# A depthwise convolution in 40 overlapping chunks, and half-sums made in another order

## The chip, the cores and the metric

The kernel runs on one core of one Trainium2 chip. TensorE (PE in the rows) multiplies matrices, VectorE (DVE) and ScalarE (ACT) read its results and do the elementwise work, GpSimd (POOL) helps and starts some of the transfers, SyncE (SP) starts the others. The metric is the device time of one execution in microseconds. Before the change it was 1102.43 us, the median of 3 runs (1102.43 to 1102.51).

## The reference

It is one layer of a streaming encoder over 640 tokens of width 1024: one prompt of 512 and 8 samples of 16, each sample with a state of its own.

```
z = x @ w_in                                    # 6656 columns: xa, ya, glu, q, three gates
out_a = (rg_lru(conv4(xa)) * gelu(ya)) @ proj_a
u = glu[..., :512] * sigmoid(glu[..., 512:])
v = causal_depthwise_conv(concat(conv_b_prev, u), conv_b_w, conv_b_b)     # 31 taps, 512 channels
out_b = silu(layer_norm(v, ln_b_g, ln_b_b)) @ proj_b
out_c = mem_cross_attention(q, k, v) @ proj_c
merged = g[0] * out_a + g[1] * out_b + g[2] * out_c
x = layer_norm(alpha * x + merged @ w_out)
x = layer_norm(alpha * x + (silu(x @ w_ffn_gate) * (x @ w_ffn_up)) @ w_ffn_down)
```

Layer norms before the layer, the memory's projections and the new states of both convolutions are computed too. The prompt's convolution starts from zeros, that of a sample from its 30 earlier rows.

## The kernel before

Activations lie with channels on the 128 partitions and the 640 tokens along the row, in the tiles `xh` and `xl`. Every product is made in three passes, since a number is kept as a high and a low part of a short format: high x high, high x low, low x high. A weight block of 128 output channels is loaded by SP's queue (`wr`), its high part is copied by ScalarE (`wh`), its low part is subtracted by VectorE (`wl`, some by POOL), and TensorE makes two 320-column accumulations of it (`pu`), which ScalarE and VectorE read.

The program is a list of such steps in a fixed order: memory projections, the GLU blocks, the queries, the gates, `proj_c`, `proj_b`, the first gate's pairs, `proj_a`, the output projection, the FFN pairs, the down projection. All compute instructions go through one helper, so their line is L64. Background streams (the convolution, attention, the LayerNorm of the second branch, the scan, the half-sums) are generators. While a step's instructions are written out, a planner sums prices for VectorE, ScalarE and TensorE (`price_vector`, L75, and its neighbours) and lets streams go on as long as VectorE and ScalarE are priced ahead of TensorE; `finish` and `flush` run a stream to its end where its result is needed. So each engine's order follows from the prices, and a cheaper price moves work of several streams.

The second branch's convolution is `conv_b_stream` (L810). For each of four blocks of 128 channels, `conv_b_taps` (L796) starts an accumulator `v` on ScalarE and then adds 30 taps on VectorE with two instructions each: one over the prompt's columns, shifted, of 511 down to 482 columns, and one of 8 x 16 columns over the samples, which lie in a history tile of 8 x 46 columns. `ln_b_stream` (L850) sums the four blocks on POOL (L853, L855), and TensorE sums over channels with a matrix of ones (`pv<-s,ones`).

The gate pairs and the FFN's gate and up projections take two 128-column blocks at once, with seven products in place of eight (`seven`, L1464; the list `PRODUCTS`, L1459). The products need four sums of quarters of x, s1 to s4, made by `sums_stream` (L1386) on VectorE, and sums of weight quarters, t1 to t4 (`Pair`, L1429). Each product is 12 matmuls of 320 columns; its `put` reads the accumulators, and `through` (L1525) applies the gate's function on ScalarE. All of s1 to s4 are finished in the hook before the second product of the first pair. Before the down projection, `before_down` (L1709) splits the first two blocks of the FFN's hidden layer into high and low parts (`split_h`, L1701), one copy on ScalarE and one subtraction on VectorE each. Tiles of 128 x 640 come from 52 slots (`Slots`, L110).

## Time and profile before

| | |
|---|---|
| median of 3 runs | 1102.43 us |
| the profiled execution | 1102.82 us |
| its span | 1101.1 us |
| TensorE busy | 1064.1 us, 97% |
| VectorE busy | 799.0 us, 73% |
| ScalarE busy | 486.9 us, 44% |
| GpSimd busy | 165.0 us, 15% |
| granted TensorE clock, mean | 0.989 |

A row of a timeline is a run of like instructions: start, duration in us, engine and line, operation, what is written from what, shape, count, and in brackets the idle time of the engine before it with the instruction that ended it. In a run the duration reaches from the first start to the last end. Names: `s` a slot's tile, `pu` and `pv` accumulators, `pb` and `pa` per-channel parameters, `wr`, `wh`, `wl` a weight block as loaded, its high and its low part. "Granted clock" is the share of TensorE's full speed that the throttle allowed in a window.

### The profile page before, as it was taken

Reading aid. Unit: us, or ns where it says so; the run is one execution under the profiler, and the core shown is the slowest. Engines: PE = TensorE matmul, PEld = TensorE weight load, DVE = VectorE, ACT = ScalarE, POOL = GpSimd, SP = SyncE. Lnnn points to the kernel's source line nnn. Section 1 sums busy time; section 2 is a strip of 40 time slices with the busy share of each in tenths; the row PEclk is TensorE's granted clock in tenths of the full one; section 3 lists DMA queues with packets and bytes.
Section 4 is the critical chain, followed back from the end, with each engine's and each line's share of the span. In section 5 each row is a group of like instructions: output and inputs, shape, how many; then the busy total and the mean of one; then the engine's idle time right before and its main releaser. Section 6 shows DMA issues by size and latency. Waiting matters only on the chain.

```text
span 1101.1 us, 16991 instructions
## 1 busy us (share of the span) xinstructions
PE 1064.1 (97%) x6827; PEld 1007.0 (91%) x6827; DVE 799.0 (73%) x1333; ACT 486.9 (44%) x861; POOL 165.0 (15%) x185
## 2 busy tenths in 40 slices
PE   8799898998999999999999999999999999999997
PEld 6699898997999999999999889899999999788886
DVE  6929898994465865699655579888887887544775
ACT  4532545445648346646423023444444443344341
POOL 3623323556200000010001120000000000100111
PEclk9999999998999999999999999999999999999999
DMA  9732123353313113212325431222233222734481
GB/s 339 252 95 78 39 67 96 118 154 94 118 39 96 59 58 115 78 44 77 115 78 172 148 120 59 71 82 78 77 95 97 77 77 86 278 115 132 165 294 39
DMA packets 80334, 123.11 MB, mean 112 GB/s; under 512 B 4075, under 2 KB 59371, under 8 KB 80256
## 3 DMA queue, kind: packets, MB, share of 16 engines
q1 hardware_dynamic: 73168, 100.36, 27.6%
q0 software_dynamic: 7088, 21.68, 6.3%
q8 instruction: 53, 0.87, 0.3%
q14 instruction: 25, 0.20, 0.1%
HBM read 112.41 MB, written 9.61 MB: 111 GB/s over the span
## 4 chain that ended last, share of the span: by engine, by line
PE 76%; DVE 14%; ACT 3%; issue 2%; POOL 2%; DMA 1%; SPq 0%; DVEq 0%; ACTq 0%; POOLq 0%
PE pu L64 67%; DVE s L64 12%; PE pv L64 9%; ACT s L64 2%; DVE wl L64 1%; ACT L64 1%; POOL s L540 1%; POOL s L541 1%; DMA s<-in_w_mem_k 0%; ACT wh L64 0%; DMA wr<-in_w_ffn_down 0%; DMA s<-in_x_prompt 0%; DVE xres L64 0%; DVE xl L64 0%; DVE mx L64 0%
## 5 line engine op out<-in xcount | busy, mean ns | idle before, releaser
L64 PE MATMUL pu<-xh,wh 128*128 128x320 f32 x1040 | 251.7, 314 | 4.6 <-ACT s L64 3.0
L64 PE MATMUL pu<-xh,wl 128*128 128x320 f32 x1040 | 246.9, 310 | 0.0
L64 ACT ACTIVATE wh<-wr 128x1024 fp32r<-128x1024 f32 (+1 forms) x149 | 135.1, 908 | 236.8 <-PE pu L64 139.0
L64 PE MATMUL pu<-xl,wh 128*128 128x320 f32 x888 | 219.4, 310 | 0.0
L64 PE MATMUL pu<-s,wh 128*128 128x320 f32 x1064 | 185.7, 310 | 1.6 <-ACT s L64 1.1
L64 PEld LDWEIGHTS pu<-xh,wh 128*128 128x128 f32 x1040 | 177.6, 189 | 9.4 <-ACT s L64 3.8
L64 PEld LDWEIGHTS pu<-xh,wl 128*128 128x128 f32 x1040 | 177.5, 189 | 0.0
L64 DVE TENSOR_TENSOR s<-s,s 128x640 fp32r<-128x640 f32 (+4 forms) x176 | 124.1, 723 | 62.4 <-ACT s L64 57.2
L64 PEld LDWEIGHTS pu<-s,wh 128*128 128x128 f32 x1064 | 163.4, 188 | 3.0 <-ACT s L64 1.7
L64 DVE TENSOR_TENSOR wl<-wr,wh 128x1024 fp32r<-128x1024 f32 (+1 forms) x100 | 114.1, 1142 | 67.6 <-ACT wh L64 67.6
L64 PEld LDWEIGHTS pu<-xl,wh 128*128 128x128 f32 x888 | 154.0, 189 | 0.6 <-DVE xl L64 0.6
L64 PE MATMUL pu<-s,wl 128*128 128x320 f32 x808 | 148.6, 311 | 2.8 <-ACT s L64 1.6
L64 DVE TENSOR_TENSOR s<-s,pu 128x320 f32<-128x320 f32 x186 | 87.8, 484 | 79.9 <-PE pu L64 77.1
L64 DVE SCALAR_TENSOR_TENSOR s<-s,pb,s 128x511 f32<-128x511 f32 (+14 forms) x240 | 130.1, 614 | 7.8 <-ACT s L64 7.8
L64 PEld LDWEIGHTS pu<-s,wl 128*128 128x128 f32 x808 | 126.6, 189 | 3.8 <-DVE s L64 1.9
L64 ACT ACTIVATE s<-s 128x640 fp32r<-128x640 f32 (+4 forms) x144 | 86.9, 628 | 97.2 <-DVE s L64 94.7
L64 PE MATMUL pu<-wh,s 128*128 128x512 f32 (+1 forms) x396 | 117.6, 390 | 3.0 <-ACT s L64 2.6
L64 PEld LDWEIGHTS pu<-wh,s 128*128 128x128 f32 x396 | 73.8, 191 | 18.2 <-ACT s L64 2.9
L64 ACT ACTIVATE s<-pu 128x320 f32<-128x320 f32 (+2 forms) x90 | 36.7, 442 | 75.5 <-PE pu L64 75.5
L64 PE MATMUL pu<-wl,s 128*128 128x512 f32 (+1 forms) x198 | 63.3, 391 | 1.5 <-POOL wl L305 0.8
L305 POOL TENSOR_TENSOR wl<-wr,wh 128x1024 fp32r<-128x1024 f32 x13 | 44.4, 3414 | 83.1 <-ACT wh L64 70.3
L64 PE MATMUL pv<-wh,s 128*128 128x512 f32 (+1 forms) x152 | 48.7, 368 | 0.4 <-DVE xres L64 0.4
(139 smaller groups left out, 1241.6 us busy)
## 6 DMA issues: line engine op xcount, KB each, us to landing
wr<-in_w_in SPq DMA_DIRECT2D x26, 1024.0 KB, 5.2
wr<-in_w_ffn_down SPq DMA_DIRECT2D x19, 1024.0 KB, 5.0
wr<-in_w_ffn_gate SPq DMA_DIRECT2D x11, 1024.0 KB, 5.4
wr<-in_w_ffn_up SPq DMA_DIRECT2D x11, 1024.0 KB, 5.4
s<-in_cache_mem_k POOLq DMA_DIRECT2D x16, 256.0 KB, 7.4
s<-in_cache_mem_v POOLq DMA_DIRECT2D x16, 256.0 KB, 6.9
wr<-in_proj_a SPq DMA_DIRECT2D x4, 1024.0 KB
wr<-in_w_out SPq DMA_DIRECT2D x4, 1024.0 KB, 5.9
```

The lines of the kernel that those rows point to most:

```text
L64: return f(*a, **k)
L305: self.eng.tensor_tensor(l, x, f32(h), op=OP.subtract)
L540: G.tensor_tensor(y[1], y[1], g[1], op=OP.mult)
L541: G.tensor_tensor(y[1], y[1], b[1], op=OP.add)
```

## The change

The history tiles become one tile per block of channels, `u0` to `u3`, of 40 chunks with 46 columns each: 32 chunks of the prompt and 8 of the samples, each with its 30 earlier columns and 16 of its own. Two memsets on POOL clear the history of the prompt's first two chunks. VectorE writes the GLU's product straight into the chunks' last 16 columns in two instructions of 20 x 16, and ScalarE copies the earlier columns: 31 x 16, 30 x 14 and, for the new states, 128 and 30 columns. A tap is then one instruction of 40 x 16 = 640 columns, so 120 instead of 240.

When a block's convolution is done, its tile is used again as three parts (`m0` to `m3` in the rows), which `get` gives out first for high and low parts; the slots go from 52 to 40.

The sums stream makes the wholes and mixtures of 22, 21 and 11 for both halves first, then the parts of s2 and s3, s1 where it does not overwrite a quarter of x, then 12 and s4. The first pair of each group takes its products in the order m1, m4, m2, m6, m7, m5, m3, with m4's `put` delayed until m7's; a product that needs a sum first calls `sum_there`, which runs the stream to that sum. The first two calls of `split_h` move from `before_down` into hooks before the fifth and fourth step from the end of the FFN pairs.

```diff
-NSLOT = 52
+NSLOT = 40
...
             def evac_a(p, k=k):
-                u = sg.pop(k)
-                each(V.tensor_mul, u, two(u), p)
-                copy(us[k][:, :, 30:46], u[:, TP:].rearrange("p (b t) -> p b t", t=TS))
-                up[k] = u
+                u = us[k]
+                for c in range(2):
+                    V.tensor_mul(u[:, 20 * c:20 * c + 20, 30:46],
+                                 *(y.rearrange("p (c n) -> p c n", n=TS) for y in (c2(sg[k])[:, c], p[c])))
+                free(sg.pop(k))
+                copy(u[:, 1:32, 14:30], u[:, 0:31, 30:46])
+                copy(u[:, 2:32, 0:14], u[:, 0:30, 32:46])
+                if k == 0:
+                    up[0] = get([128, KC, 160])
+                copy(up[0][:, k, :128].rearrange("p (b t) -> p b t", t=TS), u[:, 32:, 30:46])
+                copy(up[0][:, k, 128:158], u[:, 31, 16:46])
                 uready.append(k)
...
         for j in range(29, -1, -1):
-            s = 30 - j
-            V.scalar_tensor_tensor(v[:, s:TP], u[:, :TP - s], w(j), v[:, s:TP], op0=OP.mult, op1=OP.add)
-            V.scalar_tensor_tensor(vs, h[:, :, j:j + 16], w(j), vs, op0=OP.mult, op1=OP.add)
+            V.scalar_tensor_tensor(v3, h[:, :, j:j + 16], w(j), v3, op0=OP.mult, op1=OP.add)
             yield "v" if j else 1
...
+        yield from part("s2", "11", True)
+        yield from part("s3", "21")
+        if in_place is None:
+            yield from part("s1", "22")
+        for i in blocks:
+            whole("12", i)
+            yield "v"
+            mix("12", "12", "11", i)
+            free(a.pop(("11", i)))
+            yield "v"
+        yield from part("s4", "12")
...
+    def sum_there(n):
+
+        flush()
+        for item in list(streams):
+            while item[0][:4] == "sums" and n not in quarters:
+                try:
+                    next(item[1])
+                except StopIteration:
+                    streams.remove(item)
+                    break
+        assert n in quarters
...
-        for i, (n, u, opens, xn, wn) in enumerate(PRODUCTS):
+        products = [PRODUCTS[i] for i in ((0, 5, 2, 1, 3, 4, 6) if first else range(7))]
+        for i, (n, u, opens, xn, wn) in enumerate(products):
...
+            if first and xn[0] == "s":
+                before = lambda xn=xn: sum_there(xn)
+            elif first and i == 2 and following:
+                before = lambda: (following.sums_1(), following.sums_2())
...
-    pair_steps(pairs, lambda: finish("sums1"))
+    pair_steps(pairs)
+    for k in range(2):
+        assert steps[-5 + k].before is None
+        steps[-5 + k].before = lambda k=k: split_h(k)
...
-        for k in range(2):
-            split_h(k)
```

**The taps, on VectorE.** Before, the first block of channels begins so (`s10` is the accumulator, `s1` the prompt's columns, `s4` the samples' history, `pb` the taps' weights):

```order
L64 SCALAR_TENSOR_TENSOR s10_61_870<-s1_59_730,pb_86,s10_61_870 128x511
L64 SCALAR_TENSOR_TENSOR s10_61_870<-s4_55_687,pb_86,s10_61_870 128x128
L64 SCALAR_TENSOR_TENSOR s10_61_870<-s1_59_730,pb_86,s10_61_870 128x510
L64 SCALAR_TENSOR_TENSOR s10_61_870<-s4_55_687,pb_86,s10_61_870 128x128
L64 SCALAR_TENSOR_TENSOR s10_61_870<-s1_59_730,pb_86,s10_61_870 128x509
L64 SCALAR_TENSOR_TENSOR s10_61_870<-s4_55_687,pb_86,s10_61_870 128x128
```

After, at the same place (`u0` holds the chunks, `s7` is the accumulator, a count at the end stands for as many alike instructions; `pu` rows are the queries' results):

```order
L64 SCALAR_TENSOR_TENSOR s7_58_885<-u0_687,pb_86,s7_58_885 128x640 x6
L64 TENSOR_TENSOR s25_60_953<-pu_859,s24_59_952 128x320
L64 TENSOR_TENSOR s25_60_953<-pu_860,s24_59_952 128x320
L64 SCALAR_TENSOR_TENSOR s7_58_885<-u0_687,pb_86,s7_58_885 128x640 x8
L64 TENSOR_TENSOR s29_62_1023<-pu_922,s28_61_1022 128x320
```

Two instructions over two regions of the accumulator become one over all of it, and each reads what the one ahead of it wrote.

**The sums of the first FFN pair, on VectorE.** Before, around the last of them (the first three rows mix sums of the second half; the next four write the low parts of `s38`, `s19`, `s21` and `s8`, which are s2, s3, s1 and s4 or stand for them; the last is the put of m6):

```order
L64 TENSOR_TENSOR s19_418_7014<-s38_416_6983,s19_418_7014 128x640
L64 TENSOR_TENSOR s38_416_6983<-s21_419_7027,s38_416_6983 128x640
L64 TENSOR_TENSOR s8_417_7012<-s8_417_7012,s38_416_6983 128x640
L64 TENSOR_TENSOR s0_423_7046<-s38_416_6983,s11_422_7045 128x640
L64 TENSOR_TENSOR s45_425_7050<-s19_418_7014,s5_424_7049 128x640
L64 TENSOR_TENSOR s24_427_7054<-s21_419_7027,s29_426_7053 128x640
L64 TENSOR_TENSOR s27_429_7058<-s8_417_7012,s30_428_7057 128x640
L64 TENSOR_TENSOR wl_7037<-s16_403_6903,wl_7037 128x512
L64 TENSOR_TENSOR s41_430_7077<-wr_6886 128x512
L64 TENSOR_TENSOR s47_431_7079<-s41_430_7077,wr_6886 128x512
L64 TENSOR_TENSOR s15_420_7039<-s15_420_7039,pu_7061 128x320
```

After, between the put of m6 and that of m3 (`pu_6932` is the accumulator of m6 and m7, `pu_6888` that of m4, `pu_6973` that of m5; `m1_1722<-s8` is the low part of s1's second half, `s25` and `s38` become s4):

```order
L64 TENSOR_TENSOR s4_417_6897<-s4_417_6897,pu_6932 128x320
L64 TENSOR_TENSOR wh_6946<-wr_6533,wh_6946 128x512
L64 TENSOR_TENSOR s23_418_6898<-s4_417_6897,pu_6932 128x320
L64 TENSOR_TENSOR s39_423_6930<-s23_418_6898,pu_6888 128x320
L64 TENSOR_TENSOR m1_1722<-s8_398_6738,m0_1164 128x640
L64 TENSOR_TENSOR s25_426_6971<-xh_83,xl_84 128x640
L64 TENSOR_TENSOR wl_6964<-wr_6746,wl_6964 128x512
L64 TENSOR_TENSOR s28_427_6989<-s23_418_6898,pu_6973 128x320
L64 TENSOR_TENSOR s25_426_6971<-s25_426_6971,s14_397_6707 128x640
L64 TENSOR_TENSOR s38_428_6993<-xh_83,xl_84 128x640
L64 TENSOR_TENSOR s38_428_6993<-s38_428_6993,s5_406_6827 128x640
L64 TENSOR_TENSOR s19_430_6997<-s25_426_6971,s10_429_6996 128x640
L64 TENSOR_TENSOR s22_432_7001<-s38_428_6993,s2_431_7000 128x640
```

The second half of s1 stands behind the two puts that read m7, and s4 behind the first put that reads m5.

**The hidden layer's first parts, on ScalarE.** Before, at the end of the FFN pairs (the copies of 1024 columns are high parts of the down projection's weights, those of 640 the hidden layer's):

```order
L64 ACTIVATE wh_9627<-s23_586_9502 128x512
L64 ACTIVATE wl_9643<-wr_9397 128x512
L64 ACTIVATE wh_9662<-wr_9532 128x1024
L64 ACTIVATE wh_9682<-wr_9532 128x1024
L64 ACTIVATE wh_9703<-wr_9656 128x1024
L64 ACTIVATE s25_594_9709<-s7_402_6882 128x640
L64 ACTIVATE s44_596_9713<-s35_407_6923 128x640
```

After:

```order
L64 ACTIVATE wl_9457<-s6_582_9346 128x512
L64 ACTIVATE s23_588_9459<-s26_400_6742 128x640
L64 ACTIVATE wh_9477<-s24_583_9348 128x512
L64 ACTIVATE s17_590_9479<-s33_405_6782 128x640
L64 ACTIVATE wl_9497<-wr_9243 128x512
L64 ACTIVATE wh_9516<-wr_9378 128x1024
L64 ACTIVATE wh_9536<-wr_9378 128x1024
L64 ACTIVATE wh_9557<-wr_9510 128x1024
L64 ACTIVATE m1_1722<-s39_423_6930 128x640
```

Both copies of 640 columns that stood behind the third copy of a down weight now stand among the last pair's own.

## Rows read from the trace of the kernel before

**Rows 1.** The page, part 1: busy time and share of the span by engine.
```profile
PE 1064.1 (97%) x6827; PEld 1007.0 (91%) x6827; DVE 799.0 (73%) x1333; ACT 486.9 (44%) x861; POOL 165.0 (15%) x185
```

**Rows 2.** Timeline, TensorE: start, duration, operation, count, then idle time before, releaser.
```profile
253.69 2.50 PE L64 MATMUL pv<-s,ones 128*128 128x512 f32 x4 [5.01 <-POOL s L855]
...
499.04 2.03 PE L64 MATMUL pu<-s,wl 128*128 128x320 f32 x12 [0.68 <-DVE s L64]
...
690.66 0.42 PE L64 MATMUL pu<-s,wl 128*128 128x320 f32 x1 [1.60 <-ACT s L64]
691.52 2.24 PE L64 MATMUL pu<-s,wl 128*128 128x320 f32 x7 [0.44 <-DVE s L64]
...
940.45 1.22 PE L64 MATMUL pu<-wh,s 128*128 128x512 f32 x2 [2.63 <-ACT s L64]
```

**Rows 3.** Busy time by window: PE, PEld, DVE, ACT, POOL, granted clock, DMA share, GB/s.
```profile
254.00:256.00 2.00, 2.00 (x5) 0.97 (x5) 0.79 (x1) 1.99 (x6) 2.00 (x4) 0.50 0.45 98
692.00:694.00 2.00, 2.00 (x9) 2.00 (x9) 2.00 (x4) 1.53 (x3) 0.00 (x0) 0.50 0.00 0
942.00:944.00 2.00, 2.00 (x7) 1.58 (x6) 1.86 (x2) 0.00 (x0) 0.00 (x0) 0.53 0.91 338
```

**Rows 4.** The page, part 5: the taps of the second branch's convolution.
```profile
L64 DVE SCALAR_TENSOR_TENSOR s<-s,pb,s 128x511 f32<-128x511 f32 (+14 forms) x240 | 130.1, 614 | 7.8 <-ACT s L64 7.8
```

**Rows 5.** Timeline, VectorE, while it works through the taps.
```profile
125.03 3.78 DVE L64 SCALAR_TENSOR_TENSOR s<-s,pb,s 128x511 f32<-128x511 f32 x8 [2.87 <-ACT s L64]
...
179.15 8.58 DVE L64 SCALAR_TENSOR_TENSOR s<-s,pb,s 128x511 f32<-128x511 f32 x12 [3.74 <-ACT s L64]
...
188.98 7.40 DVE L64 SCALAR_TENSOR_TENSOR s<-s,pb,s 128x505 f32<-128x505 f32 x16
...
236.91 1.22 DVE L64 TENSOR_TENSOR wl<-wr,wh 128x1024 fp32r<-128x1024 f32 x1
238.05 13.91 DVE L64 SCALAR_TENSOR_TENSOR s<-s,pb,s 128x491 f32<-128x491 f32 x20
```

**Rows 6.** Groups by shape, VectorE: count, busy us, mean ns, idle before.
```profile
L64 DVE SCALAR_TENSOR_TENSOR s<-s,pa,s 128x128 f32<-128x128 f32 x24 | 8.3, 345 | 0.0
L64 DVE SCALAR_TENSOR_TENSOR s<-s,s 128x640 f32<-128x640 f32 x8 | 6.6, 820 | 1.8 <-ACT s L64 1.8
...
L64 DVE SCALAR_TENSOR_TENSOR s<-s,pa,s 128x511 f32<-128x511 f32 x8 | 6.0, 750 | 20.2 <-ACT s L64 20.2
```

**Rows 7.** Timeline, VectorE, ahead of and in the first FFN pair.
```profile
666.19 3.02 DVE L64 TENSOR_TENSOR s<-xh,xl 128x640 f32<-128x640 f32 x4
...
675.49 0.69 DVE L64 TENSOR_TENSOR s<-wr 128x512 f32<-128x512 f32 x1
676.21 0.69 DVE L64 TENSOR_TENSOR s<-s,wr 128x512 f32<-128x512 f32 x1
...
686.02 0.82 DVE L64 TENSOR_TENSOR s<-s,s 128x640 f32<-128x640 f32 x1
686.76 0.88 DVE L64 TENSOR_TENSOR s<-s,pu 128x320 f32<-128x320 f32 x2
```

**Rows 8.** Timeline, TensorE, in the first FFN pair and behind it.
```profile
686.55 0.31 PE L64 MATMUL pu<-xh,wh 128*128 128x320 f32 x1
...
701.43 1.93 PE L64 MATMUL pu<-s,wh 128*128 128x320 f32 x12
703.20 0.31 PE L64 MATMUL pu<-xh,wl 128*128 128x320 f32 x1
```

**Rows 9.** Timeline, ScalarE, in the first FFN pair and ahead of the down projection.
```profile
689.87 2.62 ACT L64 ACTIVATE s<-s 128x640 fp32r<-128x640 f32 x4 [0.93 <-DVE s L64]
...
700.39 0.47 ACT L64 ACTIVATE s<-s 128x320 f32<-128x320 f32 x1 [2.87 <-DVE s L64]
...
938.72 1.06 ACT L64 ACTIVATE wh<-wr 128x1024 fp32r<-128x1024 f32 x1 [5.08 <-DMA wr<-in_w_ffn_down]
```

**Rows 10.** Groups by shape, ScalarE: a copy of 128 columns.
```profile
L64 ACT ACTIVATE s<-s 128x128 f32<-128x128 f32 x12 | 3.8, 314 | 6.7 <-DVE s L64 6.7
```

More of the change, by code (lines that the diff above doesn't have):

```diff
@@ L114, in __init__ @@
         self.at = {}
+        self.parts = {}
         self.count = 0
@@ L118, in get @@
     def get(self, shape, dtype=F32):
-        if not self.free_list:
-            raise RuntimeError("no slot is free")
-        i = self.free_list.pop(0)
+        of_parts = [i for i in self.free_list if isinstance(i, tuple)]
+        if dtype == F32R and of_parts:
+            i = of_parts[0]
+        else:
+            if len(of_parts) == len(self.free_list):
+                raise RuntimeError("no slot is free")
+            i = next(i for i in self.free_list if i not in of_parts)
+        self.free_list.remove(i)
         self.low = min(self.low, len(self.free_list))
         self.count += 1
-        x = self.pool.tile([128, T], dtype, name=f"s{i}_{self.count}", tag=f"s{i}", bufs=1)
+        if isinstance(i, tuple):
+            x = self.parts[i[1]]
+        else:
+            x = self.pool.tile([128, T], dtype, name=f"s{i}_{self.count}", tag=f"s{i}", bufs=1)
         x = view(x, shape)
@@ L127, in get, with add @@
         return x
+    def add(self, tile):
+        for k in range(tile.shape[1] // T):
+            self.parts[len(self.parts)] = tile[:, k * T:(k + 1) * T]
+            self.free_list.append(("part", len(self.parts) - 1))
     def free(self, *xs):
@@ L814, in conv_b_stream @@
             yield from conv_b_taps(k)
-            free(us[k])
+            slots.add(sp.tile([128, 3 * T], F32R, name=f"m{k}", tag=f"u{k}", bufs=1))
             if k == 1:
@@ L1386, in sums_stream @@
     def sums_stream(in_place=None):
+        quarters.clear()
         for n, (t0, k0) in QUARTERS.items():
             quarters[n] = tuple([x[:, k0 + k, t0:t0 + HT] for k in range(half)] for x in (xh, xl))
[L1390 to L1412 removed]
@@ new lines, in sums_stream, with whole, mix, part @@
+        a = {}
+        def whole(n, i):
+            t0, k0 = QUARTERS[n]
+            a[n, i] = get([128, 2, HT])
+            V.tensor_tensor(a[n, i], *(f32(x[:, k0 + i:k0 + i + 2, t0:t0 + HT]) for x in (xh, xl)), op=OP.add)
+        def mix(out, p, q, i, op=OP.subtract):
+            V.tensor_tensor(a[out, i], a[p, i], a[q, i], op=op)
+        def part(n, q, keep=False):
+            at = [], []
+            for i in blocks:
+                hi, lo = get([128, 2, HT], F32R), get([128, 2, HT], F32R)
+                split(hi, lo, a[q, i])
+                if not keep:
+                    free(a.pop((q, i)))
+                sums.extend((hi, lo))
+                for to, y in zip(at, (hi, lo)):
+                    to.extend(y[:, k] for k in range(2))
+                yield "v"
+            quarters[n] = at
@@ new lines, in sums_stream @@
+        blocks = range(0, half, 2)
+        for i in blocks:
+            whole("22", i)
+            whole("21", i)
+            yield "v"
+            mix("22", "21", "22", i, OP.add)
+            whole("11", i)
+            yield "v"
+            mix("21", "11", "21", i)
+            mix("11", "22", "11", i)
+            yield "v"
+        yield from part("s2", "11", True)
+        yield from part("s3", "21")
+        if in_place is None:
+            yield from part("s1", "22")
+        for i in blocks:
+            whole("12", i)
+            yield "v"
+            mix("12", "12", "11", i)
+            free(a.pop(("11", i)))
+            yield "v"
@@ L1415, in sums_stream @@
                 yield None
-            for i, x in last:
-                hi, lo = (y[:, i:i + 2, HT:] for y in (xh, xl))
-                split(hi, lo, x)
-                free(x)
+            for i in blocks:
+                split(*(y[:, i:i + 2, HT:] for y in (xh, xl)), a["22", i])
+                free(a.pop(("22", i)))
                 yield 1
-            parts["s1"] = quarters.pop("21")
-        quarters.update(parts)
+            quarters["s1"] = quarters.pop("21")
+    def sum_there(n):
[8 more added lines that the diff above has]
+        assert n in quarters
     def sums_over():
@@ L1462, in trunk, with seven, fourth @@
     parity = [0]
-    def seven(pair, put, following, begin=None):
-        acc, tmp = {}, {}
+    def seven(pair, put, following, first=False):
+        acc, tmp, late = {}, {}, []
+        def fourth(p):
+            put(0, 1, p, tmp["b"][:, 0], OP.subtract)
         def after(n, p):
@@ L1477, in after @@
                 V.tensor_tensor(tmp["b"][:, 0], tmp["a"][:, 0], p, op=OP.add)
+                if late:
+                    fourth(late.pop())
             elif n == "m5":
@@ L1519, in pair_steps @@
         for i, (pair, put) in enumerate(pairs):
-            seven(pair, put, pairs[i + 1][0] if i + 1 < len(pairs) else None, begin if i == 0 else None)
+            seven(pair, put, pairs[i + 1][0] if i + 1 < len(pairs) else None, i == 0)
     def w_load(w, col, users):
```

62 lines of the change are left out of this document (20 added, 42 removed).

## The prediction

> **What bounds the kernel now.** I read the page's busy shares first, then the idle time on TensorE's own timeline, then what the releaser of each gap was doing. TensorE is busy 97% of the span [rows 1], so a change can win or lose only in the idle 37 us, in the slow-clock time behind gaps, or by new gaps. The gaps that touch the edited code are few [rows 2]: 5.01 us before the first sum over channels of the second branch's LayerNorm (released by POOL, which waits for the convolution's last tap), 0.68 us in the first gate pair, 1.60 and 0.44 us in the first FFN pair, and 2.63 us where the down projection starts. Behind three of them the granted clock stood at 0.50 to 0.53 of full, its 1.2 GHz level [rows 3]; those are the gaps of 5.01, 1.60 + 0.44 and 2.63 us, while none follows the 0.68. At that level two microseconds hold 9 matmuls [rows 3], 0.22 us each or more, where 0.147 is usual ((703.20 - 701.43) / 12 [rows 8]); the seven at 691.52 take 2.24 us [rows 2]. Some eleven matmuls, each about 0.14 longer, make 1.5 us of loss, and I take 1.7 for a dip with its edges.
>
> The profiled run took 1102.82 us with a span of 1101.1, so 1.7 us lie outside it; the median shown is 1102.43, 0.4 us lower. The sum below is a difference and is put on the median.
>
> **The taps.** Before, a tap is two instructions: 120 of 482 to 511 columns and 120 of 128 columns [rows 4]. Where nothing disturbs them 16 instructions, 8 taps, take 7.40 us [rows 5], 0.925 us a tap. Beside POOL work they take longer: 10 taps in 13.91 us [rows 5]. All 240 are busy for 130.1 us [rows 4]; 120 x 0.925 is 111, so about 19 us is this disturbance, and I leave it as it is, because POOL's work stays.
>
> After, a tap is one instruction of 640 columns. Nothing of that shape with a per-channel scalar is in the trace, so I bound it. A 128-column one takes 345 ns and a 511-column one 750 [rows 6], 1.057 ns a column; 640 columns give 750 + 129 x 1.057 = 886 ns. The 640-column form without the per-channel scalar takes 820 [rows 6]: the lower bound. What counts is the spacing, and there the new order matters. Four adds of 640 columns that don't need each other take 3.02 us [rows 7]: with the last at 0.82, the others start 0.73 us apart, each 0.09 before the one ahead has ended. The add at 676.21 reads what the one at 675.49 wrote: it starts 0.03 us after that one's end (675.49 + 0.69 = 676.18) [rows 7]. Before, a tap's two instructions alternate between two regions of the accumulator, so each one's forerunner is two back and they overlap (750 + 345 - 2 x 85 = 925). After, every tap reads what the one just ahead wrote. So a tap costs 0.886 + 0.03 = 0.916 us, and the 120 together save 120 x 0.009 = 1.1 us. Were they to overlap, they would start 0.80 apart and save 120 x 0.125 = 15 us. I take 1.1, since the row at 676.21 is the same situation, and keep 15 as a rival.
>
> The Trainium skill, page "VectorE: DVE Perf Modes", section "The DRAIN you can't avoid", says otherwise: each operation drains the pipe anyway, a semaphore after each of a chain costs nothing extra, and what helps is fewer operations. By it, halving the operations would give the larger saving. The two spacings above speak against it here, 0.12 us apart for dependent and independent operations.
>
> **The LayerNorm's wait (D).** The planner prices a tap at what two regions cost less one start, and so moves things: in TensorE's order the LayerNorm's first matmul has 48 matmuls fewer ahead of it. At 0.147 us each that is 7.05 us of work which now stands behind the wait instead of ahead of it. So the stretch grows by 7.05 us less what the last tap comes earlier. The last tap gains 1.1 (taps) and 1.2 (one 1024-column weight split [rows 5] moves behind it with that work). VectorE's idle time shrinks: of 2.87 us ahead of the second block of channels [rows 5] all goes, since its chunks are ready when the first block ends; I allow 2 us, an estimate, for smaller gaps that go too; the 3.74 us at the third block [rows 5] grow, since its input still waits for the GLU on TensorE: by 1.2, eight matmuls of 0.147, also an estimate. The first tap starts 1.4 later: ScalarE makes four copies, where one of 128 columns took 314 ns [rows 10]; with 0.47 us for 320 columns [rows 9], 496 and 420 columns cost about 0.61 and 0.55, and the two small ones 0.31 and 0.25: 1.72 - 0.31. Together 1.1 + 1.2 + 2.9 + 2 - 1.2 - 1.4 = 4.6, and with what the small DVE waits ahead may add, 5.5. D = 7.05 - 5.5 = +1.5 us, the dip behind it unchanged. Bounds: -7.7 (no wait left, the first rival) and +6.8 (the third).
>
> **First gate pair (A).** The sums for it are there before their products, so the 0.68 us [rows 2] go: -0.7. Bounds 0 and -0.7.
>
> **First FFN pair (B).** Unstalled, seven products end 7 x 12 x 0.147 = 12.35 us behind 686.55, at 698.9; before, they end at 703.20 [rows 8]: 4.3 us lost. After, the order of products is m1, m4, m2, m6, m7, m5, m3. The first five find what they need. But the second block of s1 stands, on VectorE and ScalarE, behind the puts of m7: two adds of 320 columns (0.88, as the pair at 686.76), a SiLU of 320 columns (0.47), the block's high part on ScalarE (0.73, since four overlapping ones take 2.62) and its low part on VectorE (0.82, as the add at 686.02) [rows 7, 9] make 2.9; m5 has 4 matmuls (0.6) to do meanwhile, so with hand-overs it waits 2.4 us. Then the sums for m3 stand behind the put of m5: the put itself 0.49, four steps of 640 columns with one overlap, 0.82 + 0.74 + 0.82 + 0.82 [rows 7], together 3.7 us, all waited for. That is 6.1, and 1.8 for one dip: 7.9 lost against 4.3, B = +3.6. Bounds: -4.3 (nothing lost) and +4.9 (two dips).
>
> **Start of the down projection (C).** Before, the first two blocks of the hidden layer are split into parts behind a weight copy on ScalarE that waits 5.08 us for its DMA [rows 9]; TensorE waits until 940.45. After, both splits stand ahead of that copy, in the last pair's steps. What is late next is that pair's last put, at about 938. So the gap of 2.63 [rows 2] falls to some 0.2, and the dip with it: -2.4 - 1.7 = -4.1. Bounds -4.3 and 0.
>
> **The rest (E).** Eight memsets on POOL, the tiles' second use as parts, 40 slots for 52: hidden by POOL's idle 85% [rows 1] and by slots that stay free; +0.3, bounds 0 and +2.
>
> The sum: -0.7 + 3.6 - 4.1 + 1.5 + 0.3 = +0.6 us, so 1103.0.
>
> **The rivals.**
> 1. The taps overlap all the same. For it: the operations are half as many. Against it: row 676.21. Then the last tap comes 14 us earlier still, nothing waits for the LayerNorm, its 5.01 us and the 1.7 of the dip go, and about 1 of the small waits ahead: D = -7.7. Time: 1102.4 - 0.7 + 3.6 - 4.1 - 7.7 + 0.3 = 1093.8.
> 2. The sums in order of need do what their order says: no product of the first FFN pair waits. For it: in the new order the two late sums have five products, 8.8 us, ahead of them. Against it: they stand behind puts that need those products. B = -4.3, time 1095.1.
> 3. Slower: a tap costs more than two did. Its runs are 16 columns long on both sides, and it stands longer beside POOL's work. Every 0.01 us a tap is 1.2 us on the last tap; at 0.96 us, D = 1.5 + 120 x 0.044 = +6.8 and the time 1108.3. It decides from 0.935 us a tap on (1105.3). Against it: the 128-column form has runs of 16 columns and no extra cost in 345 ns, and POOL's work is the same.
> 4. The edit's main part does not matter: VectorE has room at 73% [rows 1] and only C and B tell. D = 0, time 1101.5; inside the forecast's range.
>
> **How the numbers follow.** A measurement of this kernel can tell about 0.2% (2.2 us) from no change. Forecast with rival 4: 0.40, 1099.5 to 1106.5; its share below 1100.2 is 0.04, within 2.2 us 0.26, above 1104.6 0.10. Rival 1: 0.20, all faster. Rival 2: 0.14, of it 0.13 faster. Rival 3: 0.26, of it 0.24 slower and 0.02 within. Faster 0.37, same 0.29, slower 0.34. The range from 1094 to 1109 leaves out little more than half of rival 1 and the far end of rival 3.
>
> **What would show it.** Taps: in the profile after, 120 instructions of 640 columns at 0.88 to 0.92 us spacing; 0.80 means rival 1, over 0.935 rival 3. D: the gap before the LayerNorm's first matmul of 6 to 8 us instead of 5. B: a gap of about 2.4 us inside m5 and one of 3.7 ahead of m3, with a slow clock behind; no such gaps, rival 2. C: no gap of more than 0.5 us at the down projection and no fall of the clock. A: no gap in the first gate pair. The prediction is wrong if the taps' spacing or the two gaps of the FFN pair are other than this; C alone can't carry it beyond 4 us.

## The result: slower by 7.7 us, just outside the range

The changed kernel took 1110.16 us (median of 4 runs, 1109.14 to 1111.08) against 1102.43; the ratio is 1.0071, 95% interval [1.0059, 1.0083]. The forecast was 1103.0 with a range from 1094 to 1109. The profiled execution took 1109.4 us with a span of 1107.6, so 6.5 us of span are to be found (the span before was 1101.1).

The page's busy times hardly move, and the row of the taps answers to [rows 4]:

```profile
PE 1065.3 (96%) x6827; PEld 1007.2 (91%) x6827; DVE 792.5 (72%) x1213; ACT 493.9 (45%) x874; POOL 165.2 (15%) x193
...
L64 DVE SCALAR_TENSOR_TENSOR s<-u,pb,s 128x640 f32<-128x640 f32 x120 | 121.6, 1015 | 10.5 <-ACT s L64 4.5
```

TensorE does the same work; what grew is the time in which it waits or runs at the low clock. Its timeline after (start, duration, operation, count, idle time before it and releaser), beside [rows 2]:

```profile
95.47 0.81 PE L64 MATMUL pu<-xh,wh 128*128 128x320 f32 x2 [2.81 <-DVE s L64]
...
122.17 0.39 PE L64 MATMUL pv<-s,s 128*128 128x256 f32 x1 [1.49 <-DVE s L64]
...
152.10 0.81 PE L64 MATMUL pu<-xh,wh 128*128 128x320 f32 x2 [1.36 <-DVE u L64]
...
163.10 0.79 PE L64 MATMUL pu<-xh,wh 128*128 128x320 f32 x2 [2.01 <-DVE u L64]
...
190.45 5.28 PE L64 MATMUL pv<-s,s 128*128 128x256 f32 x23 [3.16 <-DVE s L64]
...
252.44 1.35 PE L64 MATMUL pv<-s,ones 128*128 128x512 f32 x4 [2.50 <-POOL s L876]
...
505.22 1.99 PE L64 MATMUL pu<-m,wh 128*128 128x320 f32 x12 [0.67 <-ACT wh L64]
...
509.64 0.82 PE L64 MATMUL pu<-m,wh 128*128 128x320 f32 x4 [0.67 <-DVE s L64]
...
699.66 2.00 PE L64 MATMUL pu<-m,wh 128*128 128x320 f32 x12 [0.67 <-DVE s L64]
...
703.88 0.41 PE L64 MATMUL pu<-m,wl 128*128 128x320 f32 x1 [1.64 <-ACT m L64]
704.74 2.02 PE L64 MATMUL pu<-m,wl 128*128 128x320 f32 x7 [0.45 <-DVE m L64]
708.85 0.63 PE L64 MATMUL pu<-s,wh 128*128 128x320 f32 x1 [2.08 <-ACT s L64]
710.41 3.30 PE L64 MATMUL pu<-s,wh 128*128 128x320 f32 x11 [0.93 <-DVE s L64]
713.51 0.47 PE L64 MATMUL pu<-xh,wl 128*128 128x320 f32 x1
...
946.98 1.93 PE L64 MATMUL pu<-s,wl 128*128 128x320 f32 x12
948.75 0.62 PE L64 MATMUL pu<-wh,s 128*128 128x512 f32 x2
```

In the kernel before, the waits of more than 1.1 us up to the LayerNorm's were, beside the 5.01 in [rows 2], the first three of these rows; the last is the last product of the FFN pairs, which stands at 946.98 after:

```profile
137.37 0.74 PE L64 MATMUL pu<-xh,wh 128*128 128x320 f32 x2 [2.50 <-ACT s L64]
...
169.46 1.09 PE L64 MATMUL pv<-ident,s 128*128 128x128 f32 x8 [1.16 <-ACT s L64]
...
188.12 3.01 PE L64 MATMUL pv<-s,s 128*128 128x256 f32 x23 [1.62 <-DVE s L64]
...
935.89 1.93 PE L64 MATMUL pu<-s,wl 128*128 128x320 f32 x12
```

The reader sees three things. The LayerNorm's wait is half as long, 2.50 us for 5.01, but ahead of it stand five others of 1.36 to 3.16 us in place of these three; the sum of all is 13.3 us after and 10.3 before. In the first FFN pair there are 5.8 us of gaps instead of 2.0. And 948.75, where the down projection starts, has no gap at all (2.63 before).

The granted clock shows the second part of the price (the columns are those of [rows 3]):

```profile
190.00:192.00 2.00, 1.55 (x7) 1.55 (x8) 2.00 (x6) 0.00 (x0) 2.00 (x4) 0.50 0.91 272
192.00:194.00 2.00, 2.00 (x11) 2.00 (x11) 1.93 (x3) 0.00 (x0) 1.32 (x2) 0.50 0.83 261
...
704.00:706.00 2.00, 1.55 (x6) 1.33 (x7) 2.00 (x3) 0.35 (x1) 0.00 (x0) 0.76 0.33 110
...
712.00:714.00 2.00, 2.00 (x9) 2.00 (x8) 0.25 (x1) 0.00 (x0) 0.00 (x0) 0.50 0.00 0
714.00:716.00 2.00, 2.00 (x11) 2.00 (x11) 1.55 (x4) 0.99 (x2) 0.00 (x0) 0.68 0.00 0
```

The engine had stood still for 3.16 us before the first of these dips, and for 0.67, 1.64 and 0.45 us before the second; its waits of 2.08 and 0.93 us came while that one lasted. At 0.50 two microseconds hold 11 matmuls of 256 columns (the attention's scores, the row at 190.45) and 9 of the FFN's. The kernel before kept the full clock behind its 1.62 us there: the same 23 matmuls took 3.01 us where they take 5.28 after, and by the window that the changed kernel spends at 0.50 it has gone on to the next products:

```profile
192.00:194.00 2.00, 2.00 (x16) 2.00 (x15) 2.00 (x5) 1.64 (x8) 0.00 (x0) 1.00 0.52 141
```

For the FFN's, 0.147 us apart [rows 8] would be 13. The second dip ends between 714 and 716, so it also slows the start of the second pair.

Where the time went, read at the same matmul in both traces:

| place | before | after | late | in this part |
|---|---|---|---|---|
| first product of the first gate pair | 492.92 | 497.35 | 4.43 | D and E: +4.4 |
| first product of the second gate pair | 506.23 | 511.47 | 5.24 | A: +0.8 |
| first product of the first FFN pair | 686.55 | 691.79 | 5.24 | 0 |
| first product of the second FFN pair | 703.20 | 713.51 | 10.31 | B: +5.1 |
| last product of the last FFN pair | 935.89 | 946.98 | 11.09 | B: +0.8 more, the end of the dip |
| span | 1101.1 | 1107.6 | 6.5 | C: -4.6 |

So B made +5.9 in all and C -4.6.

### The profile page after: what moved, and what is told of

Read it like the earlier page. It is cut to its first block, busy times and chain, and to the rows that moved or that the text cites. A ratio compares the mean times of both kernels' runs of the same rounds, so it can differ in the third digit from the quotient of the medians.

```text
span 1107.6 us, 16902 instructions
## 1 busy us (share of the span) xinstructions
PE 1065.3 (96%) x6827; PEld 1007.2 (91%) x6827; DVE 792.5 (72%) x1213; ACT 493.9 (45%) x874; POOL 165.2 (15%) x193
## 4 chain that ended last, share of the span: by engine, by line
PE 69%; DVE 2%; ACT 1%; issue 1%; DVEq 0%; ACTq 0%
PE pu L64 62%; PE pv L64 7%; DVE s L64 1%; ACT s L64 1%; DVE xres L64 0%; ACT wh L64 0%; ACT L64 0%; DVE wl L64 0%; DVE m L64 0%; DVEq L1958 0%; ACT m L64 0%; DVE st L64 0%; DVE mv L64 0%; DVE t L64 0%; DVE ve L64 0%
## 5 line engine op out<-in xcount | busy, mean ns | idle before, releaser
L64 DVE SCALAR_TENSOR_TENSOR s<-u,pb,s 128x640 f32<-128x640 f32 x120 | 121.6, 1015 | 10.5 <-ACT s L64 4.5
L64 DVE TENSOR_TENSOR s<-s,s 128x640 f32<-128x640 f32 (+4 forms) x134 | 94.1, 710 | 44.8 <-ACT s L64 37.0
L64 PE MATMUL pu<-m,wh 128*128 128x320 f32 x656 | 114.5, 311 | 3.4 <-DVE s L64 2.4
L64 PEld LDWEIGHTS pu<-m,wh 128*128 128x128 f32 x656 | 100.4, 188 | 5.7 <-ACT wh L64 1.8
L64 PE MATMUL pu<-m,wl 128*128 128x320 f32 x536 | 96.4, 311 | 2.1 <-ACT m L64 1.6
L64 PE MATMUL pu<-wh,s 128*128 128x512 f32 (+1 forms) x292 | 86.1, 389 | 0.3 <-ACT wh L64 0.3
L64 PEld LDWEIGHTS pu<-m,wl 128*128 128x128 f32 x536 | 83.5, 189 | 2.6 <-ACT m L64 1.9
L64 PE MATMUL pu<-s,wh 128*128 128x320 f32 x420 | 78.9, 315 | 3.0 <-ACT s L64 2.1
L64 PEld LDWEIGHTS pu<-s,wh 128*128 128x128 f32 x420 | 66.9, 192 | 3.8 <-ACT s L64 2.5
L64 PE MATMUL pu<-s,wl 128*128 128x320 f32 x260 | 50.9, 309 | 0.0
```

The source lines that it names most:

```text
L64: return f(*a, **k)
```

## Experiments

**The three parts alone.** The change has three parts that can be made one at a time: the convolution with its tiles and slots; the sums with the order of products; the early splits.

```diff
# e1_split: the kernel before, with
+    for k in range(2):
+        assert steps[-5 + k].before is None
+        steps[-5 + k].before = lambda k=k: split_h(k)
...
     def before_down():
         sums_over()
-        for k in range(2):
-            split_h(k)
```

> The kernel before, with only the two early splits of the hidden layer moved into the last pair. Theory: the down projection then starts without its 2.63 us gap and the slow clock behind it, whatever the rest of the change does; between the two traces this place gave back 3.7 us (10.3 late ahead of it, 6.6 behind it), so 1102.4 - 3.7 = 1098.7, between 1098 and 1099.5. Rival: what was given back belonged to the other edits (other slots, other order), and alone the gap only moves to the next block's parts: 1101 to 1102.5.

Measured: 1098.07 us, ratio 0.9959 [0.9946, 0.9973], -4.1 us against the kernel before, which took 1102.19 us beside these runs (1102.54 and 1102.52 beside the later ones). The 3.7 us of the expectation were read 0.8 us too small, as the last two rows of the table above show. The first block's matmul follows the pair's last product with no gap, and the low clock that followed before is not there:

```profile
935.65 1.93 PE L64 MATMUL pu<-s,wl 128*128 128x320 f32 x12
937.42 0.62 PE L64 MATMUL pu<-wh,s 128*128 128x512 f32 x2
```

So C stands by itself. e2_conv takes only the hunks of the convolution (`NSLOT`, `Slots`, `us`, `evac_a`, `conv_b_taps`, `conv_b_states`):

> The kernel before, with only the convolution in 40 chunks and its tiles and slots. Theory: the stretch up to the first gate pair loses 4.4 us by the two traces (492.9 to 497.4), and this comes from the taps and the order that their price gives, so 1102.4 + 4.4 = 1106.8, between 1105.5 and 1108. Rival: the 40 slots and the reused tiles hurt the pairs as well, then 1109 or more. Second rival: the prediction's own sum, +1.5 us, 1103.9.

Measured: 1105.73 us, ratio 1.0037 [1.0024, 1.0049], +3.5 us: inside the first theory's range, and neither the prediction's 1103.9 nor 1109. e3_sums takes only the hunks of `sums_stream`, `sum_there` and `seven`:

> The kernel before, with only the sums in another order and the other order of products in the first pairs. Theory: the waits of s1 and s4 behind the puts of m7 and m5 are in the order of the instructions, not in the convolution: +0.8 at the first gate pair and +5.1 at the first FFN pair, 1108.3, between 1107 and 1109. Rival: with 52 slots and the old stretch ahead VectorE is free earlier and both pairs run without a gap: 1097.5 to 1099.

Measured: 1110.13 us, ratio 1.0069 [1.0056, 1.0081], +7.9 us, more than its part of the trace (6.7); its five runs lay between 1107.23 and 1110.87, and the profiled one was the lowest. With 52 slots and the old stretch ahead the gaps in the pair are the same to a hundredth (1.64, 0.45, 2.08 and 0.93 us), so they belong to the order of the sums and products. The three parts sum to 3.5 + 7.9 - 4.1 = +7.3; the whole made +7.7.

**The price of a tap.** The planner counts 797 ns for a tap; undisturbed ones start 0.92 us apart in the trace after (the row at 132.06 below: 6.41 us for seven, the last 0.88). e4_price changes that number alone; the instructions stay, but for ScalarE's function-table loads (24 in the changed kernel, 21 here), and only their order moves with it:

```diff
# e4_price: the changed kernel, with
             V.scalar_tensor_tensor(v3, h[:, :, j:j + 16], w(j), v3, op0=OP.mult, op1=OP.add)
+            V.time += 120.0
```

> The changed kernel, the planner told 120 ns more for each tap (917 instead of 797 ns, what the trace shows undisturbed); no instruction changes, only the order. Theory: the underpriced taps put too many of them ahead of the queries' and the GLU's evacuations that TensorE waits for, so the gaps of 2.81 us at 95.5, 1.49 at 122.2 and 3.16 at 190.5 with the slow clock behind it shrink, and the time falls by 3 to 6 us, to 1104 to 1107. Rival: the loss comes from VectorE standing idle until the third block of channels can start (5.15 and 4.49 us ahead of 180.5), which a price doesn't touch: 1109 to 1111.

Measured: 1099.99 us, ratio to before 0.9984 [0.9975, 0.9992]; against the changed kernel that is -10.2 us, more than I expected, and it makes up for the sums' loss. VectorE's timeline shows a part of what an underpriced tap does; first the changed kernel, then the repriced one:

```profile
87.37 7.64 DVE L64 SCALAR_TENSOR_TENSOR s<-u,pb,s 128x640 f32<-128x640 f32 x6
94.93 0.88 DVE L64 TENSOR_TENSOR s<-pu,s 128x320 fp32r<-128x320 f32 x2
...
132.06 6.41 DVE L64 SCALAR_TENSOR_TENSOR s<-u,pb,s 128x640 f32<-128x640 f32 x7
...
139.61 8.60 DVE L64 SCALAR_TENSOR_TENSOR s<-u,pb,s 128x640 f32<-128x640 f32 x5
...
151.57 0.88 DVE L64 TENSOR_TENSOR u<-s,pu 128x320 f32<-128x320 f32 x2
...
162.47 0.88 DVE L64 TENSOR_TENSOR u<-s,pu 128x320 f32<-128x320 f32 x2
...
171.76 0.22 DVE L64 TENSOR_TENSOR s<-s,s 128x64 f32<-128x64 f32 x1 [5.15 <-POOL s L1008]
...
180.49 8.44 DVE L64 SCALAR_TENSOR_TENSOR s<-u,pb,s 128x640 f32<-128x640 f32 x7 [4.49 <-ACT s L64]
```

```profile
154.31 0.88 DVE L64 TENSOR_TENSOR u<-s,pu 128x320 f32<-128x320 f32 x2
...
174.61 8.45 DVE L64 SCALAR_TENSOR_TENSOR s<-u,pb,s 128x640 f32<-128x640 f32 x6 [2.89 <-ACT s L64]
```

And TensorE's waits in the repriced kernel:

```profile
94.04 0.81 PE L64 MATMUL pu<-xh,wh 128*128 128x320 f32 x2 [1.75 <-DVE s L64]
...
154.93 0.78 PE L64 MATMUL pu<-xh,wh 128*128 128x320 f32 x2 [1.18 <-DVE u L64]
...
183.44 3.01 PE L64 MATMUL pv<-s,s 128*128 128x256 f32 x23 [1.27 <-DVE s L64]
...
248.73 2.35 PE L64 MATMUL pv<-s,ones 128*128 128x512 f32 x4 [4.72 <-POOL s L877]
```

In the changed kernel the evacuation at 94.93, for which TensorE waits 2.81 us, stands behind the six taps of the row at 87.37; the GLU's at 151.57 and 162.47 are late as well (1.36 and 2.01 us). In `conv_b_stream` the third block stands behind all four GLU products and the new states (ScalarE copies these at 178.60 and starts the third accumulator at 179.55), so it begins late, and VectorE runs dry: it stands still 5.15 us ahead of 171.76 and 4.49 ahead of 180.49. In the repriced one the GLU's last product, at 154.31, is 8 us earlier and the third block begins at 174.61. The waits of 1.49 and 1.36 us are gone, and that of 3.16, with the dip behind it, is 1.27 without a dip; another dip stands behind the 1.75 us at 94.04 (the clock is 0.50 from 96 to 98), and the LayerNorm's wait is back at 4.72. Between the first tap's start and the last one's end VectorE stands idle 16.4 us in the changed kernel (168.11 less 151.75 busy) and 10.1 in the repriced (165.63 less 155.50). The rival of that run was half right: VectorE does stand idle for the third block, but the price sets how long.

This earlier end of the taps is the smaller part of the 10.2 us. The repriced kernel also has 1550 matmuls ahead of the LayerNorm's first, as the kernel before, where the changed one has 1502; the 48 are the 7.05 us of the prediction's D. The LayerNorm's first matmul starts 3.7 us earlier (248.73 for 252.44), so at the first product of the first gate pair the repriced kernel is 9.7 us ahead (487.66 for 497.35): 7.05 and 3.7, less the dip that is back behind the LayerNorm's wait.

e5 joins the convolution at 917 ns with the early splits; sums and products as before:

> The kernel before with the convolution in chunks at a tap price of 917 ns and the early splits; sums and products in the old order. Theory: the parts add. The repriced kernel stands 2.2 us under before although its sums cost 7.9 and its splits gave 4.1, so the convolution at the right price is worth -6.0; with the splits 1102.2 - 6.0 - 4.1 = 1092.1, between 1090.5 and 1094. Rival: the price helped by chance in that one order (it moved the first pairs too), then 1097 to 1100.

Measured: 1093.39 us, ratio 0.9918 [0.9904, 0.9931], as the theory had it. With the sums' 7.9 that makes 1101.3, where e4 measured 1099.99, so the parts add to within 1.3 us. Without the splits' 4.1 the convolution at the right price is worth -5.0, at the wrong one +3.5.

e10 and e11 are e5 with `V.time += 60.0` and `+= 240.0`; e8 and e12 are the kernel before with `V.time -= 128.0` and `+= 120.0` behind a tap's two instructions.

> The kernel before, its planner told 128 ns less for each tap (797 instead of 925 for the pair of instructions); the same instructions in another order. Theory: the price alone is what made the new convolution slower; the changed taps cost what the old ones did to 1%, so the old taps at the wrong price lose about as much as the new ones do against the right price, 9.5 us: 1107 to 1112. Rival: the loss belongs to the new form of the taps (ScalarE's copies, the third block's start, the longer single instruction beside POOL): 1101 to 1104.

> The run with the convolution and early splits that took 1093.4 us, with 857 instead of 917 ns for a tap. Theory of the price: half the error, so between 1093.4 and the 1101.6 that the same parts make at 797 ns (1105.7 less 4.1): 1095 to 1099. Rival: the order that comes out at one price is a matter of chance, and any time between 1090 and 1103 can come, 1093 as well as 1101.

> The same with 1037 ns for a tap, about what one takes with POOL beside it (mean 1.02 us). Theory of the price: the undisturbed cost is best, a higher one leaves VectorE idle before the LayerNorm and its wait grows: 1094 to 1098. Second theory: the disturbed mean is the right price, since a tap does take that: 1090 to 1093. Rival of chance: outside both.

> The kernel before, 1045 instead of 925 ns for a tap's two instructions (their mean with POOL beside them is 1.08 us). Told 128 ns too little it lost 1.3 us. If the old order was only unlucky, with its gap of 2.50 us at 137.4 and the slow clock behind it, another price removes that: 1098 to 1100. If the new form of the taps is what gave the 4.7 us that remain between the two at right prices: 1102 to 1105.

| price of a tap | new taps, early splits | old taps |
|---|---|---|
| 797 ns | 1101.6 (e2_conv less 4.1) | 1103.87 (e8) |
| 857 | 1101.1 (e10) | |
| 917, 925: about what it costs undisturbed | 1093.39 (e5) | 1102.5 (before) |
| 1037, 1045 | 1108.35 (e11) | 1109.52 (e12) |

(By `price_vector` the old pair's price goes with its length, from 925 ns at 511 columns down to 895 at 482; the figures for the old taps are those of the longest.) Of the prices tried, both columns are lowest at the undisturbed cost. Mispricing upward is dearest: in e11 streams that should have run beside the steps are not done when they are needed, and TensorE waits for them later on:

```profile
284.37 1.12 PE L64 MATMUL pv<-ident,s 128*128 128x128 f32 x4 [5.84 <-ACT s L64]
...
498.77 1.50 PE L64 MATMUL pu<-m,wl 128*128 128x320 f32 x6 [3.18 <-DVE s L64]
```

None of the four theories held here. Half the error (e10) cost almost all of it. The disturbed mean of 1.02 us is not the better price (e11). The old taps lost 1.3 us when underpriced by as much (1103.87 less 1102.54) where the new ones lose 8.2 (1101.6 less 1093.39); there the rival held, by which the wrong price is dear in the new form alone. And the old taps overpriced lost 7 us (e12), where at most 2.6 was expected. What a price does can be read at the LayerNorm's first matmul: how many matmuls stand ahead of it, and when it starts.

| run | price | matmuls ahead | last tap ends | the LayerNorm's first matmul starts | first product of the first gate pair |
|---|---|---|---|---|---|
| new taps, e2 | 797 ns | 1502 | 249.03 | 251.61 | 498.07 |
| e10 | 857 | 1502 | 249.00 | 250.74 | 497.62 |
| e5 | 917 | 1550 | 246.97 | 248.70 | 488.08 |
| e11 | 1037 | 1742 | 259.25 | 264.20 | 491.33 |
| old taps, e8 | 797 | 1502 | 245.56 | 248.14 | 495.20 |
| before | 925 | 1550 | 251.96 | 253.69 | 492.92 |
| e12 | 1045 | 1710 | 252.23 | 261.86 | 489.63 |

At 797 and 857 this matmul has the same place, so half the error costs the same 48 matmuls, 7.05 us: the price works in a step. Of the 10.0 us between e2 and e5 at the gate pair 2.9 more are the LayerNorm's later start. The underpriced old taps give up the same 48 matmuls but end 6.4 us earlier than at 925, so little is lost; why VectorE idles 16.4 us in e2 and only 11.8 in e8 stays open. Overpriced, the LayerNorm's first matmul waits for nothing, both kernels reach the gate pair earlier than the kernel before, and the loss comes behind it. No run moves this one matmul alone, so its share is read from the traces.

What is shown, then, is that the order which the price of 797 makes is what cost the new form its time: e4 changes the number and with it only the order, and the time falls by 10.2 us; e5 stands 8.2 us under the same parts at 797 ns (e2 less the splits). It isn't shown that the true cost is the best price as a rule. The rival of chance, that the order which comes out at a price is a good or a bad one by luck, was written down for e10 and e11, and both times lie where it put them.

**Dependent or independent.** e6 is e5 with the taps alternating between two accumulators, which one add joins, and the planner's old 797 ns:

```diff
# e6_two_accumulators: e5, with
+        v2 = get([128, T])
+        v4 = v2.rearrange("p (c t) -> p c t", t=TS)
+        A.activation(v4, h[:, :, 29:45], AF.Identity, scale=w(29))
...
-        for j in range(29, -1, -1):
-            V.scalar_tensor_tensor(v3, h[:, :, j:j + 16], w(j), v3, op0=OP.mult, op1=OP.add)
-            V.time += 120.0
+        for j in range(28, -1, -1):
+            y = v4 if j % 2 else v3
+            V.scalar_tensor_tensor(y, h[:, :, j:j + 16], w(j), y, op0=OP.mult, op1=OP.add)
+            if j == 0:
+                V.tensor_tensor(v, v, v2, op=OP.add)
+                free(v2)
```

> As the run before it, but taps alternate between two accumulators, so that each reads what the one two back wrote, with one more copy on ScalarE and one more add a block, and the old price of 797 ns. Theory: dependent neighbours cost 0.92 us and independent ones 0.80, so undisturbed taps are spaced 0.80 us; VectorE saves 4 x (30 x 0.92 - 29 x 0.80 - 0.82) = 14 us and the wait ahead of the LayerNorm goes: 1085 to 1090. Rival: the spacing is the same 0.92 whatever they read, then VectorE is underpriced again as in the changed kernel and the time is 1100 or more.

Measured: 1088.83 us, ratio 0.9885 [0.9868, 0.9902]. Seven undisturbed taps:

```profile
190.94 5.65 DVE L64 SCALAR_TENSOR_TENSOR s<-u,pb,s 128x640 f32<-128x640 f32 x7
```

(5.65 - 0.88) / 6 = 0.80 us apart, where the changed kernel's seven at 132.06 are (6.41 - 0.88) / 6 = 0.92 apart: the same instruction, the same operands' shapes, one reads its forerunner's output and the other doesn't. The price of 797 ns is now true, the LayerNorm's first matmul has the same place in TensorE's order as in the changed kernel, 48 matmuls earlier than before, and it waits for nothing; its row has no idle time:

```profile
238.76 1.35 PE L64 MATMUL pv<-s,ones 128*128 128x512 f32 x4
```

The first product of the first gate pair starts at 484.46 (492.92 before): the stretch gained 8.5 us where the prediction's first rival gave 7.7. At the wait in the first FFN pair it is 9.4 (681.21 for 690.66).

**The sums.** e7 draws the sums earlier, on e4. It leaves one thing out: a put that reads m6's accumulator stands behind the first matmuls of m7, which add to it, so the results of the first pairs are not the reference's.

```diff
# e7_sums_pulled: e4_price, with
     def sum_there(n):
-        flush()
...
-            if first and xn[0] == "s":
-                before = lambda xn=xn: sum_there(xn)
+            if first and i in (3, 4):
+                before = lambda ns=(("s2", "s1"), ("s3", "s4"))[i - 3]: [sum_there(n) for n in ns]
```

> The repriced kernel of the earlier run; the first pair's sums are drawn one or two products earlier (s1 ahead of m6, s4 ahead of m7) and without writing the waiting puts out first. Theory: the gaps of 1.64 + 0.45 us in m5 and 2.08 + 0.93 us ahead of m3, with the slow clock, come from the puts of m7 and m5 that stand ahead of the sums on VectorE and ScalarE; without them the pair loses under 1 us instead of 9.4: 1100.0 - 8.5 = 1091.5, between 1090 and 1093.5. Rival: VectorE has too little time in those 12 us for the six steps whatever their place, and the weights' parts come late instead: 1096 to 1100.

Measured: 1096.66 us, -3.3 against e4 and not -8.5. The waits in m5 and ahead of m3 went, and one of 3.39 us came inside m7, for the put of m6 that now stood behind the sums. The time lies in the rival's range:

```profile
694.82 1.44 PE L64 MATMUL pu<-m,wh 128*128 128x320 f32 x4 [3.39 <-DVE s L64]
```

This also showed why the changed kernel writes its puts out early: in its order m7 follows m6, and m3 follows m5, on the same accumulator. e9 keeps the old order of products on e6, where another product lies between, with the sums in order of need:

```diff
# e9_sums_old_products: e6 with the new sums_stream, and
+            if begin and i == 1:
+                before = lambda: sum_there("s2")
...
+                before = (lambda: (following.sums_2(), sum_there("s3"), sum_there("s1"))) if begin else following.sums_2
+            elif begin and i == 4:
+                before = lambda: sum_there("s4")
```

> The run with two accumulators, its sums now made in order of need but the products left in the old order m1, m6, m2, m7, m5, m4, m3; s1 is drawn ahead of m7 and s4 ahead of m5, and no put is written out early. Theory: what made the sums' order cost time was the new order of products, in which m7 follows m6 and m3 follows m5 on the same accumulator, so that a put must stand between; in the old order another product lies between and the sums can stand ahead of the puts. The gaps of 1.61 + 0.44 us at the first FFN pair and the slow clock behind them go: 1088.8 - 4 = 1084.8, between 1083.5 and 1086.5. Rival: VectorE cannot make six more steps in those 12 us whatever their place, and the weights' parts come late: 1088 to 1091.

Measured: 1088.51 us, ratio 0.9873 [0.986, 0.9887], no different from e6; the theory's 1084.8 did not come, and the rival's range is right, though what comes late is a put and not the weights' parts. One gap of 2.94 us, ahead of m3, takes the place of the two. It waits for m5's put on the same accumulator, which stands behind the last sums on VectorE:

```profile
690.61 3.54 PE L64 MATMUL pu<-s,wh 128*128 128x320 f32 x12 [2.94 <-DVE s L64]
```

```profile
686.61 2.46 DVE L64 TENSOR_TENSOR s<-s,s 128x640 f32<-128x640 f32 x3
688.98 0.48 DVE L64 TENSOR_TENSOR s<-s,pu 128x320 f32<-128x320 f32 x1
...
689.98 0.48 DVE L64 TENSOR_TENSOR s<-s,pu 128x320 f32<-128x320 f32 x1
```

From 677 to 692 VectorE has no idle time over 0.4 us in e9. The sums' order was not had for nothing there; fewer steps may be needed, which was not tried. e6 and e9 are the fastest versions, 1.2% and 1.3% under the kernel before.

## Why the prediction was wrong

The sum was +0.6 us; the two traces show +6.5. The terms that were missed are D with E (+4.4 for +1.8), A (+0.8 for -0.7) and B (+5.9 for +3.6); C gave 0.5 more than forecast.

**The taps: right undisturbed.** 0.916 us was forecast for a dependent tap, 0.92 measured; 0.80 for an independent one, 0.80 measured. The rule of the Trainium skill that was weighed there (page "VectorE: DVE Perf Modes", section "The DRAIN you can't avoid") would have had the two alike: it measured a chain of copies and found that waiting costs nothing extra. The same section also says that a next operation that isn't held starts earlier, which fits the 0.80. e6 and the changed kernel differ by 0.12 us a tap; the measurement decides. The disturbed part, which the prediction left as it was, did not stay: all taps together were busy for 130.1 us before [rows 4] and 121.6 after, 8.5 us less where 1.1 was forecast.

**D, the failing step: +1.5 forecast, +4.4 measured with E.** It said that the stretch grows by "7.05 us less what the last tap comes earlier", 5.5 us. The 48 matmuls moved as the order said, but the last tap ended at 249.86 instead of 251.96, 2.1 us earlier. The term that failed is VectorE's idle time: it was to shrink by 3.7 us (2.9 and 2 less 1.2), and between the first tap and the last it grew from 10.0 to 16.4. That VectorE's work there fell by 9.4 us (161.2 to 151.8) and not by the 2.3 that were summed for the taps and the weight split hid some 7 of these 10 us: luck, since nothing in the prediction says so. The 2 us for smaller gaps and the 0.9 of "the small DVE waits ahead" had no row behind them, and no run shows them. I had in hand a number that bears on it, a tap priced at 797 ns and costing 916, and used it only for the place of one matmul, not for the evacuations that stand behind the taps. e4 shows this part: with 120 ns more in the price the idle time is 10.1 us and the last tap ends at 247.00.

Two more things differ. POOL's last add behind the taps took 2.37 us instead of 1.53, so the LayerNorm's first matmul came only 1.25 us earlier (252.44 for 253.69). And the dip behind its wait, forecast unchanged, is gone: its first ten matmuls took 2.07 us instead of 3.90. 7.05 - 1.25 - 1.83 = 4.0; 0.4 stay for E and small waits. The forecast's sign, a gap of 6 to 8 us ahead of the LayerNorm, did not come either (2.50): TensorE itself reached that place later, behind the new waits and the dip at 190. The signs that the prediction named as deciding, the taps' spacing and the two gaps of the FFN pair, came as forecast; D's sum was not among them.

**A: -0.7 forecast, +0.8 measured.** The sums were there; but m7 (505.22) and m3 (509.64) waited 0.67 us each for the puts of m6 and m5 on the accumulators to which they add. The releaser named ahead of m7 is a weight copy on ScalarE; VectorE's put ends 0.14 us before m7 begins, as the put of m5 does ahead of m3, so it is the put as well:

```profile
504.59 0.49 DVE L64 TENSOR_TENSOR s<-s,pu 128x320 f32<-128x320 f32 x1 [1.10 <-PE pu L64]
...
509.01 0.49 DVE L64 TENSOR_TENSOR s<-s,pu 128x320 f32<-128x320 f32 x1 [0.15 <-PE pu L64]
```

The prediction did not ask which product adds to whose accumulator.

**B: +3.6 forecast, +5.9 measured.** The mechanism was right, and so were its places: 2.4 us were forecast in m5 and 1.64 + 0.45 came; 3.7 ahead of m3 and 2.08 + 0.93 came. The rows read as forecast (the two puts at 701.70, the SiLU, the parts, 3.0 us until m5 goes on):

```profile
701.70 1.01 DVE L64 TENSOR_TENSOR s<-s,pu 128x320 f32<-128x320 f32 x2 [1.58 <-PE pu L64]
703.86 0.82 DVE L64 TENSOR_TENSOR m<-s,m 128x640 fp32r<-128x640 f32 x1 [1.16 <-ACT m L64]
...
706.80 0.49 DVE L64 TENSOR_TENSOR s<-s,pu 128x320 f32<-128x320 f32 x1 [0.78 <-PE pu L64]
...
708.79 2.45 DVE L64 TENSOR_TENSOR s<-s,s 128x640 f32<-128x640 f32 x3
```

Mis-sized was the slow clock: one dip of 1.8 us was summed. It lasted from 705 to 715 and took in m5's rest, m3 and the next pair's start; 12.35 us of matmuls took 21.7, of which 5.8 are gaps, so 3.6 us are the clock, and 0.8 more are the next pair's start: 4.4 us where 1.8 were summed. The 0.67 us ahead of m7 was missing here too. The upper bound that was given, +4.9 for two dips, does not come out of its own terms, which make 5.4; the measured 5.9 lies beyond both.

**C: -4.1 forecast, -4.6 in the trace and -4.1 alone.** Right: the wait and the dip both went.

**The rivals.** The first, overlapping taps, did not come, but e6 made it, with what it gave. The second, sums that no product waits for, was wrong in every order tried. The third had the right side and the wrong mechanism: an undisturbed tap cost what was forecast, not 0.935 us or more, and the disturbed taps together cost less than before. Slower had a chance of 0.34.

## What to carry to other kernels

A planner's price is part of the program. When an instruction changes its cost, measure the new one undisturbed, dependent on its forerunner or not, and try that as the price before judging the change; here 120 ns a tap decided whether the convolution won 5.0 us or lost 3.5. Then look at what the price moved: here mostly one matmul's place, 48 matmuls earlier in TensorE's order, in one step. Halving the number of operations shortens the undisturbed chain by next to nothing (0.92 us for 0.925) if each must wait for the one ahead; two accumulators in turn brought 0.80. And where the order of accumulating products changes, list which product adds to whose accumulator: the read between them is a wait that no table of sums shows.

## What the runs showed of the hardware

- On VectorE a 640-column f32 operation with a per-channel scalar starts 0.80 us behind its forerunner if it does not need its result (e6) and 0.92 us if it does (the changed kernel).
- Runs of 16 columns, 46 apart, cost nothing extra here: a tap took 0.88 us, as the sum from the forms of 128 and 511 columns said (0.886).
- Beside POOL's subtractions of 1024 columns some taps slow, and not evenly. The five taps at 139.61 in the changed kernel take 8.60 us, and POOL splits weights for 6.05 of them. The two taps that start while these run take 2.91 and 2.92 us, each until 0.7 us behind the end of one subtraction; the other three take 0.85 to 0.89:

```profile
139.63 6.05 POOL L320 TENSOR_TENSOR wl<-wr,wh 128x1024 fp32r<-128x1024 f32 x2
```

- The length of one wait did not settle whether the granted clock fell behind it: none fell behind 2.81 us at 95.47 in the changed kernel, and one fell behind 1.75 us at 94.04 in e4 (to 0.50 from 96 to 98).
